# Entry of the two feed-forward blocks of a decoder trunk: order of the norm's sums, splits and deeper operands

## The chip, the cores and the metric

The kernel runs on one core of a Trainium2 chip. The metric is the device time of one execution in microseconds; a smaller number is better. The median of several runs is compared, and one further execution was profiled.

Names of engines: PE is the matrix engine (PEld its weight loads), DVE the vector engine, ACT the scalar engine, POOL GpSimd, SP the engine that issues most loads.

## The reference

Two layers on a residual stream x of 1024 tokens by 1024 features, all in float32. Layer 0 mixes tokens by a gated short convolution, layer 1 by attention with three dilated windows; each is followed by a SwiGLU feed-forward block with 2816 hidden features.

```python
h = rms_norm(x, mix_norm[i])
x = x + mixer(h, ...)                       # conv, then attention
h = rms_norm(x, ffn_norm[i])                # x * rsqrt(mean(x*x) + 1e-6) * gain
x = x + (silu(h @ w_gate) * (h @ w_up)) @ w_down
...
return rms_norm(x, final_norm)
```

## The kernel before

**Layout.** x is held transposed, as eight tiles X[0..7] of 128 features by 1024 tokens; a half is 512 tokens. Every float32 operand of a product is split into a high part (ACT copy, line 138) and a low part (DVE subtraction, line 139; lines 507 and 508 for the operands of the feed-forward block), and a product takes three matmuls per 128 by 128 block (hi·hi, hi·lo, lo·hi).

**Feed-forward block.** `Swiglu` multiplies the normed activations with the gate and up weights by Winograd's form of Strassen's method: seven products (u, m), m = 1..7, for each unit u of weight columns, over quarters of the activations (four feature tiles by one half of the tokens). Each product has 4 × 3 matmuls of 128 columns by 512 tokens (lines 515 to 517). The order is a written list, `unit_order` (line 252): for a feed-forward block it begins (0,1) (1,1) (0,2) (1,2) (2,1) (2,2) (3,1) (3,2) (0,6) (1,6) (0,7) (1,7) (0,4) (1,4) (0,5) (1,5) (0,3) (1,3) (2,6) ... with (3,4) as number 27. Below, "product n" is the n-th of that list. The operands of m = 1 and m = 2 need only the first half of the tokens (`first_half`, line 1061: `hcol`, line 1056, scales x by the gain and by 1/rms; then the split). Those of m = 3 to 7 need the second half too (`second_half`, line 1086, in six pieces): first the differences of scaled x tiles, times 1/rms, and so on. From unit 5 on, the products m = 2 and 4 are themselves cut by a second level of Winograd, on operands that `deepen` (line 619) prepares in some ten pieces out of the first level's (line 623 is its sums).

**What sets the order.** The program order of each engine's queue is the order in which Python emits the instructions; nothing is reordered. After product n `filled(n)` (line 766) calls `start(n)` (line 1141), then gives each of the running preparations (`deepen`) one step. Weight parts are `ops` in the order of use; `ensure(i)` (line 159) emits the loads and splits of all weights up to op i, `take` those of the product at hand and of one or two beyond.

**The entry.** The product ahead of a feed-forward block (`co`, the second half of the convolution's output projection, or `ao`, the last part of attention's) goes through `by_columns` (line 1170): first all eight output tiles for the first half of the tokens (j = 0; the first four, for `ao` five, with their products interleaved), then all eight for the second half (j = 1). After each tile: `add_to_x` (line 448) on DVE; `each`, that is `Norm.square` (line 397): ACT squares the half tile (line 408) and DVE adds the square of the tile before to `acc` (line 410); then `between` (line 1202), which saves X to DRAM, prepares weights and does these steps:

- j = 0: from tile 4 on, `ensure` of the first four weights of the feed-forward block; after tile 7 the last square is added, and DVE makes three weight sums (`combos`, line 186).
- j = 1, tile 0: `stats` part one: the column sums of `acc` on PE (line 427, eight one-column matmuls), square root on ACT (430), reciprocal and diagonal on DVE (431, 436). Tile 2: part two: spread over the partitions by PE (443) and ACT copy (444): 1/rms of the first half.
- j = 1, tiles 3 to 7: steps k = 0..7 of `first_half`, two at each of tiles 3 to 5, then one each. Each is followed by `gained(k)` (line 1073): ACT writes gain · x of the second half over the first half of X[k]; four differences of these (line 1084) are made on DVE.

In the feed-forward block `start` does the rest: product 0: end of `first_half`; 1: three sums and weights up to op (3,1); 2: `stats` part one for the second half; 3: part two and the first piece of `second_half`; 7, 8, 9, 11, 12: its other pieces. `deepen(2)` starts after product 12, `deepen(4)` after product 22 (lines 771, 773).

**End of attention.** `finish` (line 1473) divides the heads' outputs o by their sums z. For all pairs of heads but the last, z goes through DRAM, so that the reciprocal is of a 128 by 16 tile. For the last pair, DVE takes reciprocals of z in four pieces of 128 by 256 (line 1492), multiplies (1493), and splits each half of the tokens; this stands directly ahead of `ao`.

## Time and profile before

| | |
|---|---|
| median of 3 runs | 2200.58 us (2198.46 to 2203.82) |
| profiled execution | 2203.5 us, of which the profiled span is 2201.7 us |
| mean granted PE clock | 0.987 of full speed |
| feed-forward entry, layer 0 | about 305 to 420 us of the span |
| feed-forward entry, layer 1 | about 1485 to 1620 us |

A row of the timeline has the start, the duration, the engine, the line, the operation, output and inputs, and in brackets how long the engine had been idle before and what ended that. DVE instructions of one row overlap a little: 128 by 512 sums last 0.68 us and start every 0.60 us. A row of the windows view has for each stretch of the span the busy time of each engine with its count of instructions, the granted PE clock and the share and rate of the DMA engines.

### The profile page before, as it was taken

What the parts mean: (1) busy time and instruction counts of PE and PEld (TensorE: products, weight loads), DVE (VectorE), ACT (ScalarE), POOL (GpSimd) and SP (SyncE); (2) the same over time, 40 slices, a digit from 0 to 9 for tenths busy, and PEclk for the clock granted to TensorE, in tenths of its full rate; (3) what the DMA queues carried; (4) which work ended last, traced back from release to release, by engine and by line L of the source; (5) the groups of instructions that cost most, each with busy time, mean ns of one, the idle gap of its engine ahead of it and who ended that gap; (6) DMA issues with size and microseconds to landing.
All of it is one profiled execution on the core that took longest, in us unless ns stands there. A gap on an engine that the chain in (4) does not pass through costs nothing.

```text
span 2201.7 us, 30568 instructions
## 1 busy us (share of the span) xinstructions
PE 2143.2 (97%) x11158; PEld 1832.0 (83%) x11158; DVE 1762.2 (80%) x3242; ACT 997.6 (45%) x1800; POOL 153.2 (7%) x202
## 2 busy tenths in 40 slices
PE   9999999899999999999999999998899999999998
PEld 7788877688888878878999998887778888878887
DVE  7898759888888798865677777868988888889886
ACT  7433426444444444435455455534544444454435
POOL 1000000010101000010111111110010101000000
PEclk9999999999999999999999999999899999999999
DMA  7222631223333374323333333443123333265432
GB/s 222 82 91 68 224 121 39 91 96 106 110 97 119 123 280 147 113 67 130 91 91 92 94 98 89 153 148 132 53 79 105 104 105 112 96 233 198 158 91 77
DMA packets 132560, 260.03 MB, mean 118 GB/s; under 512 B 47530, under 2 KB 58810, under 8 KB 132410
## 3 DMA queue, kind: packets, MB, share of 16 engines
q1 hardware_dynamic: 76410, 186.38, 26.6%
q0 software_dynamic: 14832, 48.60, 6.4%
q10 hardware_dynamic: 41168, 23.10, 3.7%
q8 instruction: 88, 1.44, 0.3%
q14 instruction: 62, 0.51, 0.1%
HBM read 188.62 MB, written 66.26 MB: 116 GB/s over the span
## 4 chain that ended last, share of the span: by engine, by line
PE 80%; DVE 11%; ACT 4%; DMA 3%; issue 2%; ACTq 0%; SPq 0%; DVEq 0%
PE bank L517 16%; PE bank L515 16%; PE bank L516 16%; PE bank L356 5%; PE bank L358 5%; PE bank L357 5%; PE bank L1446 4%; PE bank L609 2%; PE bank L610 2%; PE bank L607 2%; DVE w L139 1%; DVE b L508 1%; PE bank L1374 1%; PE bank L1373 1%; DVE x L448 1%
## 5 line engine op out<-in xcount | busy, mean ns | idle before, releaser
L515 PE MATMUL bank<-b,w 128*128 128x512 f32 x1784 | 703.9, 395 | 14.3 <-ACT b L507 6.0
L517 PE MATMUL bank<-b,w 128*128 128x512 f32 x1784 | 702.1, 394 | 15.6 <-DVE w L139 15.6
L516 PE MATMUL bank<-b,w 128*128 128x512 f32 x1784 | 701.5, 393 | 2.6 <-DVE b L508 2.1
L517 PEld LDWEIGHTS bank<-b,w 128*128 128x128 f32 x1784 | 338.9, 190 | 91.0 <-DVE w L139 20.3
L515 PEld LDWEIGHTS bank<-b,w 128*128 128x128 f32 x1784 | 339.2, 190 | 88.5 <-ACT w L138 7.5
L516 PEld LDWEIGHTS bank<-b,w 128*128 128x128 f32 x1784 | 339.0, 190 | 73.8 <-DVE b L508 2.9
L138 ACT ACTIVATE w<-combo 128x512 fp32r<-128x512 f32 (+2 forms) x464 | 235.1, 535 | 289.2 <-DVE combo L186 280.2
L139 DVE TENSOR_TENSOR w<-combo,w 128x512 fp32r<-128x512 f32 (+2 forms) x464 | 261.3, 576 | 74.6 <-ACT w L138 71.9
L521 ACT ACTIVATE part<-bank 128x512 f32<-128x512 f32 x168 | 99.5, 595 | 271.9 <-PE bank L517 268.0
L139 DVE TENSOR_TENSOR w<-raw,w 128x512 fp32r<-128x512 f32 (+2 forms) x316 | 169.2, 561 | 21.1 <-ACT w L138 19.4
L525 DVE TENSOR_TENSOR part<-part,bank 128x256 f32<-128x256 f32 (+1 forms) x348 | 159.3, 488 | 28.9 <-PE bank L517 17.1
L138 ACT ACTIVATE w<-raw 128x512 fp32r<-128x512 f32 (+2 forms) x316 | 150.1, 520 | 45.5 <-PE bank L517 11.4
L736 DVE TENSOR_TENSOR x<-x,bank 128x512 f32<-128x512 f32 x168 | 114.6, 682 | 31.2 <-PE bank L517 31.2
L356 PE MATMUL bank<-w_hi,w 128*128 128x512 f32 (+1 forms) x320 | 121.5, 380 | 0.0
L358 PE MATMUL bank<-w_hi,w 128*128 128x512 f32 (+1 forms) x320 | 119.5, 373 | 0.7 <-DVE w L139 0.7
L357 PE MATMUL bank<-w_lo,w 128*128 128x512 f32 (+1 forms) x320 | 119.6, 374 | 0.0
L448 DVE TENSOR_TENSOR x<-x,bank 128x512 f32<-128x512 f32 (+1 forms) x104 | 66.0, 642 | 62.0 <-PE bank L358 53.0
L356 PE MATMUL bank<-h_hi,w_hi 128*128 128x512 f32 x256 | 104.6, 408 | 0.6 <-ACT w_hi L138 0.6
L186 DVE TENSOR_TENSOR combo<-raw 128x512 f32<-128x512 f32 (+1 forms) x160 | 103.2, 645 | 0.0
L358 PE MATMUL bank<-h_hi,w_lo 128*128 128x512 f32 x256 | 100.1, 391 | 0.8 <-DVE w_lo L139 0.8
L357 PE MATMUL bank<-h_lo,w_hi 128*128 128x512 f32 x256 | 99.9, 390 | 0.0
L1132 ACT ACTIVATE part<-part 128x512 f32<-128x512 f32 x66 | 39.7, 628 | 111.5 <-DVE part L525 111.5
(243 smaller groups left out, 3841.3 us busy)
## 6 DMA issues: line engine op xcount, KB each, us to landing
hin<-part SPq DMA_DIRECT2D x126, 256.0 KB
raw<-in_ffn_w_gate SPq DMA_DIRECT2D x44, 512.0 KB
raw<-in_ffn_w_up SPq DMA_DIRECT2D x44, 512.0 KB
part<-sum POOLq DMA_DIRECT2D x72, 256.0 KB, 3.0
raw<-in_ffn_w_down SPq DMA_DIRECT2D x48, 384.0 KB
raw<-in_conv_w_in SPq DMA_DIRECT2D x24, 512.0 KB
x<-spill SPq DMA_DIRECT2D x24, 512.0 KB
raw<-in_attn_w_qkv SPq DMA_DIRECT2D x24, 512.0 KB
```

Of the source, the lines that this page charges most:

```text
L138: nc.scalar.activation(hi, src, AF.Copy)
L139: eng.tensor_tensor(out=lo, in0=src, in1=hi, op=ALU.subtract)
L186: eng.tensor_tensor(out=c, in0=a, in1=b, op=op)
L356: nc.tensor.matmul(b, whi[:, a], ahi[:, s], start=first, stop=False)
L357: nc.tensor.matmul(b, whi[:, a], alo[:, s], start=False, stop=False)
L358: nc.tensor.matmul(b, wlo[:, a], ahi[:, s], start=False, stop=last)
L515: nc.tensor.matmul(b, hi[:, a], bhi, start=start and k == 0, stop=False, skip_group_check=True)
L516: nc.tensor.matmul(b, hi[:, a], blo, start=False, stop=False, skip_group_check=True)
L517: nc.tensor.matmul(b, lo[:, a], bhi, start=False, stop=k == n - 1, skip_group_check=True)
L521: nc.scalar.activation(t, b, AF.Copy)
L525: nc.vector.tensor_tensor(out=t, in0=t, in1=b, op=ALU.add)
L736: nc.vector.tensor_tensor(out=X[n][:, half(h)], in0=X[n][:, half(h)], in1=b, op=ALU.add)
```

## The change

It touches the entry of both feed-forward blocks and the end of attention.

1. `Norm.chained` takes the place of `Norm.square` there. Tile 0's square goes to `acc`, tile 1's to a second sum `odd`; those of tiles 2 and 3 are added to these two by accumulating DMAs on the POOL queue; those of tiles 4 to 7, and `odd`, by DVE: five DVE sums instead of seven in each half.
2. A new hook `added` runs between `add_to_x` and the square: the weights are split ahead of the square of the same tile, and two more (ops 4 and 5) are split in j = 1.
3. The three sums `combos` after j = 0 move behind part one of `stats`; part two moves from tile 2 to tile 1 of j = 1, and the steps of `first_half` become 0, 1, (2, 3), 4, 5, 6, 7 at tiles 1 to 7.
4. `gained` writes −gain · x for tiles 0 to 3 (the new constant `less`), and an accumulating DMA on the POOL queue adds tile k + 4 to tile k: the four DVE differences go.
5. `start`: each of the first steps moves ahead by one product, the pieces of `second_half` to products 2, 5, 7, 8, 9, 11. An activation on a scratch column asks for the Silu table after product 2; another for the Sqrt table at tile 4 of j = 0 (layer 1 only).
6. `deepen(2)` starts after product 17 (was 12), `deepen(4)` after 26 (was 22).
7. `finish`, last pair: the first half of the tokens as before; the second half's z goes to DRAM, comes back as 128 by 8, is inverted, goes to DRAM and is spread back, by five DMAs of the POOL queue; its multiplication and split (`last_part`) are emitted after tile 3 of `ao`, j = 0.

```diff
         def chained(self, k, c0, c1):
+            ...
+            if k == 1:
+                self.odd = half_page("acc2")
+            to = half_page("sq") if k > 1 else self.odd if k else acc
+            nc.scalar.activation(to, X[k][:, s], AF.Square)
+            add = lambda t: nc.vector.tensor_tensor(out=acc, in0=acc, in1=t, op=ALU.add)
+            if k in (2, 3):
+                nc.gpsimd.dma_start(out=(acc, self.odd)[k % 2], in_=to, accum_op=ALU.add)
+            if k == KT - 2:
+                self.flush()
+                add(self.odd)
+                self.odd = None
+            if k > 3:
+                self.flush()
+                self.put_off = lambda: add(to)
...
-                    if n == i - 15:
+                    if n == i - 10:
                         prep.append(self.deepen(2))
-                    if n == i - 5:
+                    if n == i - 1:
                         prep.append(self.deepen(4))
...
-            nc.scalar.activation(t, X[n][:, half(1)], AF.Identity, scale=self.norm.gain(n))
+            scale = (self.norm.gain(n), less[:, self.norm.g, n:n + 1])[n < 4]
+            nc.scalar.activation(t, X[n][:, half(1)], AF.Identity, scale=scale)
             self.xg[n] = t
-            if n > 4:
-                self.difference(n - 5)
+            if n > 3:
+                self.xd[n - 4] = self.xg[n - 4]
+                nc.gpsimd.dma_start(out=self.xd[n - 4], in_=t, accum_op=ALU.add)
...
                 if n == 0:
                     last_step()
-                elif n == 1:
                     for m in (6, 7):
                         combos[self.key, 1](m)
                     ensure(self.at(3, 1))
-                elif n == 2:
+                elif n == 1:
                     next(stats)
                     ensure(self.at(0, 6))
-                elif n == 3:
+                elif n == 2:
                     run(stats)
-                    ensure(self.at(1, 6))
                     prep.append(self.second_half())
                     next(prep[0])
-                elif n == 6:
+                    nc.scalar.activation(scratch, eps, AF.Silu)
+                    ensure(self.at(1, 6))
+                elif n == 4:
                     ensure(self.at(1, 7))
-                elif n in (7, 8, 9, 11, 12):
+                elif n in (5, 7, 8, 9, 11):
                     next(prep[0], None)
...
+            def added(j, n):
+
+                if j == 0 and n > 3:
+                    if n + 2 < KT:
+                        ensure(op_state[1] + 1)
+                    ensure(first_op + n - 4)
+                elif j and n < 2:
+                    ensure(first_op + n + 4)
...
                     if n == 3:
                         load_raw(raw_base[i] + 3)
-                    elif n > 3:
-                        ensure(first_op + n - 4)
-                    if n == KT - 1:
+                        if not i:
+                            nc.scalar.activation(less, gains, AF.Copy, scale=-1.0)
+                        if last_part:
+                            last_part.pop()()
+                    elif n == KT - 1:
                         norm.flush()
...
-                    for k in ((0, 1), (2, 3), (4, 5), (6,), (7,))[n - 3]:
+                    for k in ((0,), (1,), (2, 3), (4,), (5,), (6,), (7,))[n - 1]:
                         step(k)
...
+            nc.gpsimd.dma_start(wide(zd), z[0:65:64, HALF:])
+            zc = scope["pool"].tile([128, 8], F32, name="zl", tag="zl", bufs=1)
+            nc.gpsimd.dma_start(zc, thin(zd))
+            ...
+            for c in (0, 256):
+                nc.vector.reciprocal(z[:, c:c + 256], z[:, c:c + 256])
+                scaled(c, c + 256)
+                if c:
+                    parts(0)
                 yield
+            def rest():
+                scaled(HALF, S)
+                parts(1)
+            last_part.append(rest)
+            yield
+            nc.vector.reciprocal(zc, zc)
+            nc.gpsimd.dma_start(thin(rd), zc)
+            for a in range(2):
+                nc.gpsimd.dma_start(z[64 * a:64 * a + 64, HALF:],
+                                    bass.AP(rd.tensor, rd.offset + a * HALF, [[0, 64], [1, HALF]]))
+            yield
```

More of the change, by code (lines that the diff above doesn't have):

```diff
@@ L120, in trunk @@
     gains = consts.tile([128, 5, KT], F32)
+    less = consts.tile([128, 5, KT], F32)
     taps = consts.tile([128, KT, 3], F32)
@@ L418, in add, with chained @@
             self.square(k)
+        def chained(self, k, c0, c1):
+            s = slice(c0, c1)
+            if self.acc is None:
+                self.acc, self.rstd = page("acc"), page("rstd")
+            acc = self.acc[:, s]
+            if k == 1:
[12 more added lines that the diff above has]
+                self.put_off = lambda: add(to)
         def stats(self, c0, c1):
@@ L1168, in feed_forward, with by_columns @@
                 after(n)
-    def by_columns(key, ks, acts, pieces, each, between, wide=4, ahead=1):
+    def by_columns(key, ks, acts, pieces, each, between, wide=4, ahead=1, added=lambda i, n: None):
         w = {}
@@ L1185, in by_columns @@
                 add_to_x(n, banks[n])
+                added(i, n)
                 each(n, piece)
@@ L1206, in between @@
                         load_raw(raw_base[i] + 3)
-                    elif n > 3:
-                        ensure(first_op + n - 4)
-                    if n == KT - 1:
+                        if not i:
[3 more added lines that the diff above has]
+                    elif n == KT - 1:
                         norm.flush()
-                        for m in (6, 7):
-                            combos[i, 0](m)
-                    return
-                if n == 0:
+                    elif n == 4 and i:
+                        nc.scalar.activation(scratch, eps, AF.Sqrt)
+                elif n == 0:
                     pre.append(norm.stats(0, HALF))
                     next(pre[0])
-                if n == 2:
-                    run(pre.pop())
-                    pre.append(sw.first_half())
-                elif n > 2:
-                    for k in ((0, 1), (2, 3), (4, 5), (6,), (7,))[n - 3]:
+                    for m in (6, 7):
+                        combos[i, 0](m)
+                else:
+                    if n == 1:
+                        run(pre.pop())
+                        pre.append(sw.first_half())
+                    for k in ((0,), (1,), (2, 3), (4,), (5,), (6,), (7,))[n - 1]:
                         step(k)
-            by_columns((key, 1), ks, acts, HALVES,
-                       lambda n, c: norm.square(n, *c, eng=nc.vector), between,
-                       AO_WIDE if key == "ao" else 4)
+            by_columns((key, 1), ks, acts, HALVES, lambda n, c: norm.chained(n, *c), between,
+                       AO_WIDE if key == "ao" else 4, added=added)
         def last_step():
@@ L1230, in last_step @@
             norm.flush()
-            sw.difference(3)
         return sw, group1, norm.stats(HALF, S), last_step
@@ L1664, in trunk @@
         nc.tensor.matmul(warm[:, :128], ones, ones, start=True, stop=True)
+    last_part = []
     with tc.tile_pool(name="first", bufs=1) as scope["pool"]:
```

19 lines of the change are left out of this document (8 added, 11 removed).

## The prediction, written before the changed kernel was run

> **What bounds the kernel now.** I read the page first: its span, its table of engines and the shares of the chain that ended last.
>
> ```profile
> span 2201.7 us, 30568 instructions
> PE 2143.2 (97%) x11158; PEld 1832.0 (83%) x11158; DVE 1762.2 (80%) x3242; ACT 997.6 (45%) x1800; POOL 153.2 (7%) x202
> PE 80%; DVE 11%; ACT 4%; DMA 3%; issue 2%; ACTq 0%; SPq 0%; DVEq 0%
> ```
>
> PE bounds nearly everything: it idles 58.5 us in all. A change at two entries can win only what PE loses there, so the windows view over both comes second (busy time and count of PE, PEld, DVE, ACT, POOL, then the granted PE clock and DMA).
>
> ```profile
> 320.00:340.00 20.00, 18.67 (x77) 14.75 (x76) 12.94 (x21) 7.64 (x14) 0.00 (x0) 0.91 0.21 80
> 340.00:360.00 20.00, 18.76 (x85) 14.85 (x84) 18.77 (x33) 13.12 (x24) 0.00 (x0) 1.00 0.11 41
> 360.00:380.00 20.00, 20.00 (x90) 16.57 (x89) 19.84 (x33) 11.80 (x21) 0.00 (x0) 1.00 0.09 26
> 380.00:400.00 20.00, 14.35 (x55) 10.74 (x54) 18.92 (x35) 10.42 (x18) 1.62 (x3) 0.91 0.36 119
> 400.00:420.00 20.00, 16.42 (x64) 12.79 (x63) 18.12 (x31) 7.15 (x15) 2.69 (x5) 0.91 0.21 72
> 420.00:440.00 20.00, 20.00 (x89) 16.53 (x89) 15.77 (x29) 8.84 (x16) 0.96 (x2) 1.00 0.16 61
> 440.00:460.00 20.00, 20.00 (x89) 16.33 (x88) 17.33 (x33) 8.57 (x18) 2.27 (x5) 1.00 0.27 92
> ...
> 1500.00:1520.00 20.00, 15.58 (x63) 12.74 (x63) 14.90 (x25) 9.06 (x16) 0.00 (x0) 0.83 0.50 170
> 1520.00:1540.00 20.00, 19.08 (x83) 15.11 (x81) 17.32 (x28) 13.10 (x22) 0.00 (x0) 1.00 0.22 82
> 1540.00:1560.00 20.00, 18.83 (x70) 14.99 (x71) 17.15 (x30) 11.75 (x22) 0.00 (x0) 0.83 0.03 11
> 1560.00:1580.00 20.00, 18.46 (x82) 14.98 (x81) 19.07 (x32) 11.87 (x21) 0.00 (x0) 1.00 0.17 54
> 1580.00:1600.00 20.00, 15.95 (x57) 12.26 (x56) 19.14 (x36) 7.70 (x14) 2.17 (x4) 0.83 0.30 105
> 1600.00:1620.00 20.00, 17.53 (x71) 13.98 (x70) 15.80 (x29) 8.03 (x16) 2.16 (x4) 0.91 0.30 106
> ```
>
> Three readings. PE idles 1.33 + 1.24 + 5.65 + 3.58 = 11.8 us in entry 0 and 4.42 + 0.92 + 1.17 + 1.54 + 4.05 + 2.47 = 14.6 in entry 1. The clock is down by 3 × 0.09 × 20 = 5.4 us and (3 × 0.17 + 0.09) × 20 = 12.0. Together 43.8 us: the most there is to win. And DVE is at 18 to 20 of 20 just where PE idles, while at 420 to 460, at 15.8 and 17.3, PE has no gap. These are backlogs of DVE, each with an idle stretch of DVE ahead of it (12.9 at 320).
>
> The timeline gives the single gaps (in brackets):
>
> ```profile
> 321.75 1.05 PE L427 MATMUL bank<-ones,acc 128*128 128x1 f32 x8 [1.33 <-DVE acc L410]
> 392.30 0.50 PE L515 MATMUL bank<-b,w 128*128 128x512 f32 x1 [1.69 <-ACT w L138]
> 395.38 0.80 PE L517 MATMUL bank<-b,w 128*128 128x512 f32 x1 [2.35 <-DVE w L139]
> 395.98 0.63 PE L515 MATMUL bank<-b,w 128*128 128x512 f32 x1
> 396.41 0.63 PE L516 MATMUL bank<-b,w 128*128 128x512 f32 x1
> 414.67 0.50 PE L517 MATMUL bank<-b,w 128*128 128x512 f32 x1 [2.78 <-DVE w L139]
> ...
> 1513.46 1.87 PE L427 MATMUL bank<-ones,acc 128*128 128x1 f32 x8 [4.42 <-DVE acc L410]
> 1540.93 0.50 PE L516 MATMUL bank<-b,w 128*128 128x512 f32 x1 [1.85 <-DVE b L508]
> ```
>
> After the 2.35 gap matmuls start every 0.43 us; in the unbroken 20 us at 360 there are 90, one per 0.22 (0.227 from start to start in the timeline, used below). After the 1.69 gap they do not slow. So a gap somewhat above 2 us, or several close together, costs the clock too: this trace's rule, which I use for what stays.
>
> The Trainium skill, page "TensorE: Matmul & The Clock Gate", section "Part 1: The HAM clock gate", names about 3.4 us of idleness before the clock is halved. The trace disagrees: 2.35 us was enough. By the page only the 4.42 gap would take the clock with it (rival C).
>
> **The change part by part.** First the sums of j = 0:
>
> ```profile
> 313.30 0.68 DVE L448 TENSOR_TENSOR x<-x,bank 128x512 f32<-128x512 f32 x1
> 313.90 0.69 DVE L410 TENSOR_TENSOR acc<-acc,sq 128x512 f32<-128x512 f32 x1
> 315.26 0.69 DVE L139 TENSOR_TENSOR w<-raw,w 128x512 fp32r<-128x512 f32 x1 [0.68 <-ACT w L138]
> 315.87 0.68 DVE L448 TENSOR_TENSOR x<-x,bank 128x512 f32<-128x512 f32 x1
> ```
>
> A sum occupies DVE 0.60 us (313.30 to 313.90). A tile takes 2.57, of which 0.68 waits for ACT, whose split stands behind the square; PE makes a tile in 12 × 0.227 = 2.72, so DVE never catches up the 1.2 us it is behind. With the split ahead of the square the 0.68 goes: x, w, one sum is 1.8, with `odd` 2.4. PE was ready for L427 at 321.75 − 1.33 = 320.4, hence it had tile 7 at 317.7; tile 7's x, w and two sums end at 317.7 + 4 × 0.6 = 320.1. The 1.33 gap goes, with the slow clock behind it. ACT's queue now has the split ahead of the square, so late raw weights would hold the squares and the sums too; at 0.6 of each for ACT per 2.72 us there is room, and the raw tiles of these ops are loaded from tile 3 on as before. `less` is one ACT instruction in the same room.
>
> Entry 1 has the same chain, with 9 × 0.227 = 2.04 us per tile, and ahead of it the reciprocals:
>
> ```profile
> 1484.89 1.75 DVE L1492 RECIPROCAL z<-z 128x256 f32<-128x256 f32 x1
> 1486.74 0.42 DVE L1493 TENSOR_TENSOR o<-o,z 128x256 f32<-128x256 f32 x1
> 1516.61 1.28 ACT L430 ACT_TABLE_LOAD   x1
> ```
>
> Two reciprocals and multiplications (2 × 2.19) leave DVE before tile 0, but one multiplication and a split come back between tiles 3 and 4 (0.6, 0.6 waiting for ACT, 0.6), and the Sqrt table (1.28) now lies on ACT between tile 4's square and tile 5's split. PE was ready for L427 at 1513.46 − 4.42 = 1509.0; counting tiles back, it has tile 3 at 1500.2 (tiles 0 to 4 are interleaved, 0.68 apart). DVE: x3 to 1500.8, that detour to 1502.6, x4 and two splits to 1504.4, x5 to 1505.0. ACT, after x4 at 1503.2, has a square, the table, a root and a split, 0.6 + 1.3 + 0.3 + 0.6: 1506.0. Then DVE again: w, sum (1507.2), x, w, sum, odd (1509.6), x, w, two sums: 1512.0. The wait falls from 4.42 to 3.1 and keeps its slow clock (0.17 × 20): 3.1 + 3.4 = 6.5 us of loss stay here. From the chain of 1/rms itself the table load goes.
>
> The accumulating DMAs have no twin of their size. Bounds:
>
> ```profile
> acc<-sq POOLq DMA_DIRECT2D x6, 512.0 KB, 5.1
> part<-sum POOLq DMA_DIRECT2D x72, 256.0 KB, 3.0
> ```
>
> The first accumulates twice the bytes, the second copies the same; I take 5.1, the same operation. The POOL queue is empty in these windows (0.00), so nothing else is passed. Tile 2's square ends at about 307.5 and is needed at 314; in entry 1 at 1500.7 and 1506.6: both land in time, the second by 0.8. A late one would hold DVE at tile 5's sum, behind it x of tile 6, and with that a bank that PE needs. z's two trips are four hops in a row from 1484.9 on, when the first reciprocal has its z: at 3.0 each they end at 1496.9, at 5.1 at 1505.3; `rest` needs z at 1500.8. I take 3.0, since these hops copy and are smaller; at 5.1 DVE and all tiles behind it wait 4.5 us.
>
> Next the first half's norm and the first products. In entry 1 the column sums end at 1513.7 (1.7, as slow as in their row) and the diagonal at 1514.9. From there DVE has three weight sums, 7 x, 1 w, 8 hcol, 8 splits, 5 square sums: 24 × 0.60, and 8 a little dearer (gain and 1/rms in one, 0.66) = 19.7, so 1534.6, 1535.1 with what it waits for 1/rms. PE, from 1513.7: a slow tile, the spread, six tiles and two products = 3.3 + 0.9 + 12.2 + 5.4, so 1535.5. By 0.4 us neither L427 nor product 2 waits: the 1.85 at 1540.93 and the clock of its window go; in entry 0, with 2.72 a tile for PE, all the more, so the 1.24 idle at 340 to 360 goes too. At DVE a wait of L443's diagonal holds back only weight sums and x, which PE does not need at once.
>
> Last, the backlog in `second_half`, entry 0:
>
> ```profile
> 351.72 0.68 DVE L410 TENSOR_TENSOR acc<-acc,sq 128x512 f32<-128x512 f32 x1
> 360.54 2.49 DVE L1088 TENSOR_TENSOR x<-x,rstd 128x512 f32<-128x512 f32 x4
> 385.25 1.28 ACT L1132 ACT_TABLE_LOAD   x1 [1.43 <-issue]
> 392.70 1.42 DVE L623 TENSOR_TENSOR deep<-b 128x256 f32<-128x256 f32 x4
> 413.93 0.69 DVE L139 TENSOR_TENSOR w<-combo,w 128x512 fp32r<-128x512 f32 x1
> ```
>
> The last square sum, at 351.7, comes about 7 sooner: PE 3.1 (gap and clock), two sums 1.2, three differences 1.8, two early steps of `first_half` 1.9, less 1.0 waiting for PE. The weight splits of ops 4 and 5 fall into the 7 us that DVE idles at 320 to 340. Two splits and the fourth difference, 1.8, then make `second_half` start 8.8 sooner (360.54 to 351.7). `deepen(2)` is ten sums and splits of quarter width (0.34, by the row of four) and seven of full width: 7.6. Before, 5.7 of it preceded the split at 413.93, for product 20; now 1.3, so 4.4 move behind it. Silu's table load, which held up DVE behind ACT, comes right after 1/rms now and frees 0.6. In all 13.8: the split ends at 400.8. PE without gaps and slow clock is there at 414.67 − 11.8 − 3.6 = 399.3. So 1.5 of the 2.78 stays. `deepen(2)`'s other pieces now fall to products 18 to 24, where I leave as much again, and one slow window (1.8): 4.8 per entry, the same for entry 1. `deepen(4)` moves by four products, 11 us, into 440 to 460, where DVE had 2.7 of 20 us left: between 0 and its whole 7.6; I take 0, since its first user is product 37 and its last piece falls to product 33.
>
> Sum: 43.8 − 6.5 − 2 × 4.8 = 27.7. The profiled execution took 2203.5, so 2175.8; the median of the runs, 2200.6, is 2.9 below it, so **2173**.
>
> **The rivals.** B: DVE has no more room than the work taken from it. Four square sums and four differences per entry, 8 × 0.6 × 2 = 9.6, and 4.4 − 1.2 for the reciprocals: 12.8, so 2187.8. For it: 18 to 20 busy of 20 where PE idles. Against: DVE has 7 us idle at 320 to 340, and work moves there. A variant lets the late `deepen(4)` give back its 7.6 and a slow window of 1.8 per entry: 2173 + 19 = 2192.
>
> C: the clock does not come back with the short gaps. Then 26.4 − 3.1 − 4 × 1.5 = 17.3 of idleness is won alone: 2183.3. Against it: 360 to 380, no gap and clock 1.00.
>
> D, slower: the accumulates wait for DVE. The four differences enter the queue a tile of PE, 2.7 us, apart; the last, at about 344.4, beside the last square sum, is needed at 351.7. Its first user, product 8, comes 5 × 2.72 = 13.6 after 1/rms, and DVE needs 8.2 of these (4 scalings, 4 sums, 4 splits, 1.0 for ACT), so PE has 5.4 more. One behind another at T each they hurt by 4T − 3 × 2.7 − 7.3 − 5.4 = 4T − 20.8 per entry; with T = 12 that is 27, so 2173 + 54 = 2227. It eats the whole gain, 13.9 an entry, from T = 8.7 on. Against it: 3.0 and 5.1 were measured, the 3.0 in stretches where DVE had up to 19 of 20.
>
> The Trainium skill speaks for D: page "SBUF — State Buffer", section "A bandwidth-pool intuition that's wrong", has a POOL-issued DMA take 3100 ns instead of 620 while a DVE copy holds the shared port. No such stretch shows in the rows above.
>
> E: the change doesn't do what it says: every gap closed reappears at a later product: 2200.6.
>
> **How the numbers follow.** Forecast 0.62, B with its variant 0.24, C 0.03, E 0.05, D 0.06. A measurement tells 0.3% (6.6 us) from no change: faster 0.89, same 0.05, slower 0.06. The range runs from 2160, where the 16.1 us of loss that I leave shrink to 3, to B's 2192; it leaves out D, E and a little below: one in eight.
>
> **What would show it.** Right: no wait at L427 in entry 0 and 2 to 4 us in entry 1; none at L443; differences landing before L1088 starts; PE gaps of `w` at products 20 to 24 of at most 2 us; granted clock 1.00 from 1540 to 1580. Wrong: DVE waiting for a POOL-queue DMA (sums, differences or z), gaps at products 26 to 40, or PE idling as long as before with DVE at 19 of 20.

## The result, and the profile after

| | before | changed | |
|---|---|---|---|
| median (range), us | 2200.32 (2198.46 to 2203.82) | 2185.55 (2183.18 to 2186.07) | ratio 0.9929, 95% 0.9917 to 0.9942 |
| profiled execution's span, us | 2201.7 | 2184.3 | 17.4 less |

The kernel became 14.8 us faster; the forecast was 27.7 (2173). The lines of the page for the changed kernel that answer to those of before, the first with the span, then the engines, then the chain:

```profile
span 2184.3 us, 30619 instructions
PE 2134.3 (98%) x11158; PEld 1825.1 (84%) x11158; DVE 1750.1 (80%) x3224; ACT 999.7 (46%) x1804; POOL 169.8 (8%) x223
PE 78%; DVE 10%; ACT 4%; DMA 3%; issue 3%; ACTq 0%; SPq 0%; POOL 0%; DVEq 0%; POOLq 0%
```

PE still bounds it, and idles 50.0 us instead of 58.5. The windows of the changed kernel (busy time and count of PE, PEld, DVE, ACT, POOL, then PE's granted clock and DMA):

```profile
320.00:340.00 20.00, 20.00 (x88) 16.18 (x87) 17.34 (x28) 12.46 (x21) 3.38 (x4) 1.00 0.50 138
340.00:360.00 20.00, 20.00 (x91) 16.29 (x90) 18.10 (x32) 13.88 (x25) 1.69 (x2) 1.00 0.21 46
...
380.00:400.00 20.00, 18.09 (x79) 14.28 (x78) 19.07 (x34) 7.01 (x12) 4.40 (x8) 0.99 0.46 157
400.00:420.00 20.00, 20.00 (x84) 16.38 (x83) 15.44 (x28) 8.97 (x18) 0.45 (x1) 0.93 0.17 54
420.00:440.00 20.00, 19.06 (x84) 15.27 (x83) 18.35 (x34) 7.45 (x14) 2.80 (x6) 1.00 0.20 79
440.00:460.00 20.00, 17.74 (x104) 15.44 (x103) 16.81 (x40) 9.40 (x24) 0.54 (x1) 1.00 0.21 66
...
1480.00:1500.00 20.00, 17.63 (x78) 14.27 (x76) 11.33 (x20) 8.94 (x15) 4.02 (x6) 1.00 0.59 189
1500.00:1520.00 20.00, 16.75 (x65) 13.68 (x66) 16.99 (x28) 11.62 (x21) 1.68 (x2) 0.83 0.37 113
1520.00:1540.00 20.00, 18.85 (x86) 15.08 (x84) 18.67 (x32) 12.99 (x23) 3.36 (x4) 1.00 0.40 93
1540.00:1560.00 20.00, 19.44 (x85) 15.60 (x84) 20.00 (x34) 13.89 (x25) 0.00 (x0) 1.00 0.09 27
1560.00:1580.00 20.00, 20.00 (x88) 16.18 (x88) 19.00 (x31) 8.48 (x15) 3.60 (x7) 1.00 0.43 140
1580.00:1600.00 20.00, 18.09 (x73) 14.44 (x73) 15.85 (x31) 9.00 (x17) 0.80 (x2) 0.91 0.28 97
1600.00:1620.00 20.00, 19.06 (x84) 15.45 (x83) 19.33 (x35) 5.86 (x10) 3.25 (x6) 1.00 0.20 79
1620.00:1640.00 20.00, 17.74 (x98) 15.05 (x98) 16.02 (x37) 11.15 (x27) 0.54 (x1) 1.00 0.16 45
```

320 to 360, where PE idled and slowed before, is full at clock 1.00. New holes stand at 440 to 460 and 1620 to 1640, which were full. The timeline of the changed kernel names each gap (in brackets, with what ended it); lines moved by the change: L427 is L449, L443 is L465, L139 is L140, L515 to L517 are L537 to L539.

```profile
375.17 0.50 PE L539 MATMUL bank<-b,w 128*128 128x512 f32 x1 [0.55 <-DVE w L140]
399.40 0.75 PE L539 MATMUL bank<-b,w 128*128 128x512 f32 x1 [1.91 <-DVE w L140]
432.17 0.50 PE L539 MATMUL bank<-b,w 128*128 128x512 f32 x1 [0.94 <-DVE w L140]
448.01 0.50 PE L537 MATMUL bank<-b,w 128*128 128x512 f32 x1 [2.26 <-ACT part L543]
...
1503.25 1.01 PE L449 MATMUL bank<-ones,acc 128*128 128x1 f32 x4 [5.63 <-DVE acc L431]
1528.78 1.05 PE L449 MATMUL bank<-ones,acc 128*128 128x1 f32 x8 [1.15 <-DVE acc L431]
...
1583.47 0.50 PE L539 MATMUL bank<-b,w 128*128 128x512 f32 x1 [1.91 <-DVE w L140]
```

Counted in matmuls, the first four are products 12, 20, 31 and 36 (the expectations below call the third 34). Entry 1 repeats them (0.56, 1.91, 0.94, 2.26). With the clock's loss the entries now lose 5.66 + 1.6 (entry 0) and 12.44 + 5.2 (entry 1): 24.9 us, where the forecast left 16.1. Below, "first wait" and "second wait" are PE's waits for the column sums (L449) of the first and the second half of the tokens.

### The profile page after: what moved, and what is told of

Read it like the earlier page. It is cut to its first block, busy times and chain, and to the rows that moved or that the text cites. A ratio compares the mean times of both kernels' runs of the same rounds, so it can differ in the third digit from the quotient of the medians.

```text
span 2184.3 us, 30619 instructions
## 1 busy us (share of the span) xinstructions
PE 2134.3 (98%) x11158; PEld 1825.1 (84%) x11158; DVE 1750.1 (80%) x3224; ACT 999.7 (46%) x1804; POOL 169.8 (8%) x223
## 4 chain that ended last, share of the span: by engine, by line
PE 78%; DVE 10%; ACT 4%; DMA 3%; issue 3%; ACTq 0%; SPq 0%; POOL 0%; DVEq 0%; POOLq 0%
PE bank L537 15%; PE bank L539 15%; PE bank L538 15%; PE bank L359 5%; PE bank L357 5%; PE bank L358 5%; PE bank L1477 4%; PE bank L631 3%; PE bank L632 3%; PE bank L629 3%; DVE w L140 2%; PE bank L1405 1%; PE bank L1404 1%; DVE b L530 1%; DVE combo L187 1%
## 5 line engine op out<-in xcount | busy, mean ns | idle before, releaser
L537 PE MATMUL bank<-b,w 128*128 128x512 f32 x1784 | 702.9, 394 | 13.8 <-ACT part L543 6.6
L539 PE MATMUL bank<-b,w 128*128 128x512 f32 x1784 | 699.2, 392 | 9.3 <-DVE w L140 9.3
L537 PEld LDWEIGHTS bank<-b,w 128*128 128x128 f32 x1784 | 337.7, 189 | 88.3 <-ACT part L543 9.3
L539 PEld LDWEIGHTS bank<-b,w 128*128 128x128 f32 x1784 | 337.5, 189 | 84.7 <-DVE w L140 13.8
L139 ACT ACTIVATE w<-combo 128x512 fp32r<-128x512 f32 (+2 forms) x464 | 234.8, 535 | 291.8 <-DVE combo L187 282.8
L140 DVE TENSOR_TENSOR w<-combo,w 128x512 fp32r<-128x512 f32 (+2 forms) x464 | 261.0, 576 | 60.0 <-ACT w L139 57.6
L140 DVE TENSOR_TENSOR w<-raw,w 128x512 fp32r<-128x512 f32 (+2 forms) x316 | 169.4, 561 | 16.3 <-ACT w L139 14.8
L139 ACT ACTIVATE w<-raw 128x512 fp32r<-128x512 f32 (+2 forms) x316 | 150.7, 519 | 46.6 <-PE bank L539 13.6
```

The costliest lines, as they stand in the source:

```text
L139: nc.scalar.activation(hi, src, AF.Copy)
L140: eng.tensor_tensor(out=lo, in0=src, in1=hi, op=ALU.subtract)
L537: nc.tensor.matmul(b, hi[:, a], bhi, start=start and k == 0, stop=False, skip_group_check=True)
L539: nc.tensor.matmul(b, lo[:, a], bhi, start=False, stop=k == n - 1, skip_group_check=True)
```

## The experiments

Each edits the changed kernel alone and was timed in rounds beside the kernel before, whose median stayed between 2199.7 and 2201.4. One edited kernel's runs spread over 1.2 to 5.2 us, so I read nothing from under 2 us of difference to the changed kernel. That kernel was not timed again in these rounds: beside runs 5 to 8 the kernel before was 1.0 us slower than beside the changed kernel, so their last column may be 1 us too high.

| run | median (range), us | ratio to before (95%) | to the changed kernel |
|---|---|---|---|
| 1 deepen(4) back | 2179.96 (2179.57 to 2180.78) | 0.9909 (0.9895 to 0.9922) | -5.6 |
| 2 both deepens back | 2184.31 (2180.49 to 2185.17) | 0.9924 (0.9912 to 0.9936) | -1.2 |
| 3 z on DVE | 2184.54 (2183.84 to 2185.18) | 0.9930 (0.9916 to 0.9943) | -1.0 |
| 4 sums of tiles 2, 3 on DVE | 2187.16 (2183.15 to 2188.31) | 0.9937 (0.9924 to 0.9949) | +1.6 |
| 5 both 3 and 4 | 2183.19 (2181.56 to 2184.97) | 0.9918 (0.9905 to 0.9932) | -2.4 |
| 6 root's table earlier | 2185.37 (2183.45 to 2186.14) | 0.9926 (0.9914 to 0.9939) | -0.2 |
| 7 split behind the square | 2188.08 (2185.09 to 2188.61) | 0.9936 (0.9922 to 0.9949) | +2.5 |
| 8 differences on DVE | 2190.68 (2189.18 to 2190.93) | 0.9950 (0.9937 to 0.9962) | +5.1 |
| 9 first half's norm later | 2187.94 (2185.99 to 2189.75) | 0.9947 (0.9935 to 0.9960) | +2.4 |
| 10 high part a step ahead | 2182.31 (2180.73 to 2183.07) | 0.9921 (0.9907 to 0.9934) | -3.2 |
| 11 five edits together | 2176.63 (2174.60 to 2179.68) | 0.9893 (0.9878 to 0.9908) | -8.9 |
| 12 and two more | 2170.07 (2169.12 to 2171.73) | 0.9861 (0.9845 to 0.9878) | -15.5 |

**1 and 2: the deepen steps.** In `filled`:

```
-                    if n == i - 1:
+                    if n == i - 5:
                         prep.append(self.deepen(4))
```

> Edit: the changed kernel, with deepen(4) started at product 22 (index of the op less 5) again, as before the change; all else stays changed. Theory A (the 10 us that the forecast missed lie for the most part in deepen(4), moved by four products onto the early sums of unit 5): the waits of 0.94 and 2.26 us at products 34 to 36 of both entries go, at most 1.5 us per entry comes back at products 22 to 28, so 2 x 3.2 less 0 to 3: 3.4 to 6.4 us faster than the changed kernel, 2179 to 2182 us. Rival B (VectorE simply has no more room; the wait goes wherever deepen(4)'s 7.6 us are put): the same 3.2 per entry reappear as waits for w before product 30, time 2185 +- 2.

Run 2 also sets `i - 10` back to `i - 15` for `deepen(2)`.

> Edit: the changed kernel, with both deepen(2) (index less 15) and deepen(4) (index less 5) started where they were before the change. It prices the move of deepen(2) against the run with deepen(4) alone moved back. Theory A (the sooner sums and 1/rms gave VectorE 9 us ahead of product 12, so that deepen(2) would have had room in its old place for the most part): 4.4 us of its work return ahead of product 20's weights, the wait there grows from 1.9 us to 4 to 6 us with slow matmuls behind it, so 2 to 4 us per entry slower than with deepen(4) alone moved back: 2184 to 2190 us. Rival B (no room at all): all 4.4 us and a second slow window (1.8) per entry come back, about 12 us slower than that run: 2191 us or more.

The timeline of run 1, entry 0 from product 20 on, and the window that follows it:

```profile
399.33 0.50 PE L539 MATMUL bank<-b,w 128*128 128x512 f32 x1 [1.92 <-DVE w L140]
419.39 0.50 PE L539 MATMUL bank<-b,w 128*128 128x512 f32 x1 [0.71 <-DVE w L140]
424.05 0.50 PE L539 MATMUL bank<-b,w 128*128 128x512 f32 x1 [1.64 <-DVE w L140]
```

```profile
400.00:420.00 20.00, 19.29 (x86) 15.63 (x85) 17.61 (x35) 9.44 (x18) 0.00 (x0) 1.00 0.17 54
```

The 0.94 and 2.26 are gone, 0.71 and 1.64 stand in their place: theory A in the time, but 2.35 us per entry came back where it allowed 1.5. Of the 5.6 us by the medians, the two entries account for 3.5 in the profiles (1.9 idle time, 1.6 slow clock); the rest lies outside them, where the edit changes nothing (table below). `deepen(4)`'s move was a loss, then: 0.85 us of idleness an entry in these gaps, and the clock that goes with them. Run 2 is 4.4 slower than run 1, at A's end of the range: moving `deepen(2)` paid. Its product 20 waited 2.79 us, not the expected 4 to 6; products 15 to 17 waited 1.10, 1.20 and 0.86 ahead of it.

**3, 4, 5, 6: what holds entry 1's first column sums.** Run 3 puts `finish`'s old loop over four reciprocals back. Run 4:

```
             if k in (2, 3):
-                nc.gpsimd.dma_start(out=(acc, self.odd)[k % 2], in_=to, accum_op=ALU.add)
+                self.flush()
+                tgt = (acc, self.odd)[k % 2]
+                self.put_off = lambda: nc.vector.tensor_tensor(out=tgt, in0=tgt, in1=to, op=ALU.add)
```

> Edit: the changed kernel, with the last pair's z by four reciprocals of VectorE over 256 columns, as before the change; no DMAs of z, nothing left for between tiles 3 and 4. VectorE does two reciprocals more (1.75 each) before tile 0, and loses the waits for z's hops and the detour. Theory A (the hops came too late for the gain that they were to bring, and the detour between tiles 3 and 4 costs what the reciprocals cost): the first wait for the column sums in entry 1 is 5.6 +- 1.5 us, time 2185 +- 2. The forecast's own sum (hops in time, 4.4 less 1.2 us of VectorE saved): 3 us slower, 2188 to 2189. Rival (the late hops and the SWDGE traffic beside them are what holds the entry): the first wait falls below 4.4 us, 1.5 us or more faster.

> Edit: the changed kernel, with the sums of tiles 2 and 3 (squares) on VectorE instead of two accumulating DMAs, in both entries. It adds 2 x 0.60 us of VectorE per entry. Theory A (in entry 1 VectorE waited 0.77 and 0.59 us for these two DMAs, as much as the two sums take): entry 1's first wait 5.6 +- 0.7; entry 0's first wait comes back by at most 1.2; so 0 to 2 us slower than the changed kernel, 2185 to 2188. Rival D (the accumulating DMAs are what holds the entry): first wait of entry 1 below 4.5 us, 1 us or more faster.

Run 3's first wait is 6.26 us: taking the reciprocals off DVE was worth nothing measurable. Its timeline shows why, with the first of DVE's sums, that of tile 4's square, standing behind one DMA:

```profile
1495.51 0.69 DVE L431 TENSOR_TENSOR acc<-acc,sq 128x512 f32<-128x512 f32 x1 [3.56 <-DMA acc<-sq]
```

The changed kernel's DVE waits at both of these places too:

```profile
1496.82 0.69 DVE L431 TENSOR_TENSOR acc<-acc,sq 128x512 f32<-128x512 f32 x1 [0.77 <-DMA acc<-sq]
1499.91 0.69 DVE L431 TENSOR_TENSOR acc<-acc,acc 128x512 f32<-128x512 f32 x1 [0.59 <-DMA acc<-sq]
```

In that kernel the same transfers, in entry 0 (300 to 330; the third is the second half's) and in entry 1 (1475 to 1505), by its DMA issues (the last number is the median us to landing):

```profile
acc<-sq POOLq DMA_DIRECT2D x3, 256.0 KB, 3.2
```

```profile
acc<-sq POOLq DMA_DIRECT2D x2, 256.0 KB, 8.2
```

The second pair is late, and in run 3, without z's hops, took 8.0 as well: z's traffic is not what delays it. Run 4's first wait fell to 4.46, below what A allowed and just inside rival D's bound of 4.5, but the second rose from 1.15 to 2.35, and the time did not fall. Entry 0 shows no wait for these sums on DVE or PE in either kernel. So run 5 took both back:

> Edit: the changed kernel, with both the last pair's z (four reciprocals) and the sums of tiles 2 and 3 on VectorE; the deepen steps stay as changed. In the run with z alone on VectorE entry 1's first wait was 6.26 us, and VectorE waited 3.56 us for an accumulating DMA in it (the two took 8 us and more there). Theory A2 (in entry 1 the POOL-queue transfers, run beside the loads and spills, come later than the 3.0 to 5.1 us that the forecast took, and give back what they save VectorE): entry 1's first wait is 6.26 - 3.56 + 2 x 0.6 = 3.9 +- 0.6 us, the second 1.2 to 2.4; 1 to 3 us faster than the changed kernel (2185), 2182 to 2184. Rival B (VectorE's amount of work decides, and six operations come back to it): first wait 6 us or more, 2187 or more.

First wait 2.63 (A2: 3.3 to 4.5), second 2.77 (A2: 1.2 to 2.4): more was won at the first and more lost at the second than A2 said. The time is as A2 had it, though its 2.4 us hardly exceed the spread. What ended DVE's last wait there was the split behind the root's table load. Run 6 moved that load alone in the changed kernel:

```
             last_part.append(rest)
+            nc.scalar.activation(scratch, eps, AF.Sqrt)
             yield
```

> Edit: the changed kernel, with entry 1's early square root (the one that loads its table, 1.28 us on ScalarE) issued after the split of o's first half, where ScalarE idles 8 us, instead of behind tile 4's square. Theory A2 (that load held VectorE 1.07 us for a split, in the chain that ends at the first column sums): the first wait falls from 5.63 by 0.5 to 1.1 us, if the accumulating DMA, for which VectorE waited 0.77 right behind it, does not simply take its place; time 2184 to 2185. Rival (the DMA takes its place): first wait 5.3 or more, no change.

The DMA took its place: DVE waited 1.53 us for `acc<-sq` instead of 1.07 + 0.77, first wait 5.26, time unchanged. The rival (5.3 or more) held.

**7, 8, 9: parts that paid.** Run 7 swaps two calls in `by_columns`, so the next weights' split follows the square:

```
-                added(i, n)
                 each(n, piece)
+                added(i, n)
```

> Edit: the changed kernel, with the next weights' split issued behind the tile's square again instead of ahead of it. The forecast's own step (0.68 us of VectorE per tile waits for ScalarE when the split stands behind the square): from tile 4 on VectorE waits 0.68 per tile again; entry 0: a tile takes 2.5 (3.1 with the odd sum) against TensorE's 2.72, so the first wait comes back at 0.7 to 1.3 us; entry 1 (2.04 a tile): 4 x 0.68 less what lies in the waits for the accumulating DMAs (1.4), first wait 6.3 to 8.3 us. Time 2186 to 2189. Rival (the order is worth nothing, since the deferred sums fill that wait): no wait in entry 0, 5.6 in entry 1, 2185 +- 1.5.

Entry 0's first wait came back at 1.16 us, as the forecast's chain said; entry 1's stayed at 5.64 (expected 6.3 to 8.3): there DVE still waits 1.07 and 0.35 us for the DMAs, and for ACT twice (1.11 and 0.61) instead of at each of four tiles. Run 8 gives `gained` its old subtraction on DVE:

> Edit: the changed kernel, with the four differences of each entry on VectorE again (gains without the sign) instead of accumulating DMAs. It adds 4 x 0.60 us of VectorE per entry ahead of product 8. The forecast's step (they were 1.8 us, with the last one 2.4, of the backlog ahead of product 20): the wait at product 20 grows from 1.9 us by 1.8 to 2.4 us per entry, and product 13's from 0.55; 3 to 5 us slower than the changed kernel, 2188 to 2190. Rival D (the DMAs are what is late): no change or faster, 2185 or less.

The time nearly agrees (2190.7), the place does not:

```profile
344.03 1.05 PE L449 MATMUL bank<-ones,acc 128*128 128x1 f32 x8 [1.04 <-DVE acc L431]
...
400.31 0.50 PE L539 MATMUL bank<-b,w 128*128 128x512 f32 x1 [1.91 <-DVE w L140]
...
1531.01 1.87 PE L449 MATMUL bank<-ones,acc 128*128 128x1 f32 x8 [3.31 <-DVE acc L431]
```

Product 20 still waits 1.91. The 2.4 us of DVE work went to the second half's column sums (0 and 1.15 in the changed kernel). Run 9 moves the first half's 1/rms behind tile 2 and `first_half` to tile 3 on:

```
-                    if n == 1:
+                    if n == 2:
                         run(pre.pop())
                         pre.append(sw.first_half())
-                    for k in ((0,), (1,), (2, 3), (4,), (5,), (6,), (7,))[n - 1]:
-                        step(k)
+                    if n > 2:
+                        for k in ((0, 1), (2, 3), (4, 5), (6,), (7,))[n - 3]:
+                            step(k)
```

> Edit: the changed kernel, with the first half's 1/rms spread behind tile 2 of the second half (instead of tile 1) and first_half's eight steps from tile 3 on in their old groups (2, 2, 2, 1, 1). It moves about 1.9 us of VectorE's work per entry (the two early steps) behind the point where TensorE waits for the second half's column sums. Theory A2 (in entry 1 VectorE has no idle left between the two column sums; the run with the differences on VectorE shows what such work costs: +1.8 gave waits of 1.04 and 3.31 us there instead of 0 and 1.15): entry 0's second wait about 1, entry 1's 3.0 +- 0.5, product 20's unchanged at 1.9; 3 to 6 us slower than the changed kernel, 2188 to 2191. The forecast's own chain puts the 1.9 us into the backlog ahead of product 20: that wait 3.8 us instead of 1.9. Rival (VectorE's 2.7 us of idleness at 320 to 340 takes it): 2185 +- 1.5, nothing changes.

Second waits 0.55 and 3.14, product 20 at 1.95: A2's place again, and 2187.9, just under its range.

**10: is it the splits that make the later `deepen(4)` hurt?** Splits in `deepen` are cut: `parts` issues ACT's copies and returns DVE's subtractions, which run one step later:

```
-            d[6] = parts(t2, "half" if m == 2 else "page")
-            yield
-            d[7] = parts(t3, "page")
+            d[6], low = parts(t2, "half" if m == 2 else "page")
+            yield
+            low()
+            d[7], low = parts(t3, "page")
...
```

> Edit: the changed kernel, with the splits of the deepen pieces cut in two: ScalarE's high part is issued in one step, VectorE's low part one product later; the places of both deepens stay as changed. In the changed kernel VectorE waits 11.8 us in all for ScalarE in 12 such splits (none before the change, 5.5 with deepen(4) alone moved back): the high part stands on ScalarE behind an activation that itself waits for a sum of VectorE. Theory S (this wait, and not the 7.6 us of deepen(4)'s work, is what the later place costs, and what the forecast took as 0): VectorE's wait falls from 11.8 to below 3 us, the 2.26 us at product 36 falls below 1.3, 3 to 6 us faster than the changed kernel, 2179 to 2182. Rival W (the work itself collides with the eight early sums of unit 5): the waits at products 34 and 36 stay above 2.5 us together, 2184 to 2186.

The groups by line show DVE's part of these twelve splits (busy, mean ns | idle before them, and what ended it): before the change, in the changed kernel, in run 1 and in run 10.

```profile
L139 DVE TENSOR_TENSOR t<-deep,t 128x512 fp32r<-128x512 f32 x12 | 8.2, 684 | 0.0
```

```profile
L140 DVE TENSOR_TENSOR t<-deep,t 128x512 fp32r<-128x512 f32 x12 | 8.3, 691 | 11.8 <-ACT t L139 11.8
```

```profile
L140 DVE TENSOR_TENSOR t<-deep,t 128x512 fp32r<-128x512 f32 x12 | 8.2, 687 | 5.5 <-ACT t L139 5.5
```

```profile
L645 DVE TENSOR_TENSOR t<-deep,t 128x512 fp32r<-128x512 f32 x12 | 8.2, 685 | 0.0
```

In the changed kernel they cost DVE a microsecond each on average. Two rows of its timeline show one case: ACT itself has just waited for one of DVE's sums, and DVE then waits for the high part that ACT makes next:

```profile
445.20 0.63 ACT L1152 ACTIVATE part<-part 128x512 f32<-128x512 f32 x1 [4.72 <-DVE part L547]
446.38 0.69 DVE L140 TENSOR_TENSOR t<-deep,t 128x512 fp32r<-128x512 f32 x1 [1.22 <-ACT t L139]
```

Cutting the split takes all 11.8 us from these twelve splits, but not from DVE. The weights' splits of the same width, first in the changed kernel, then in run 10:

```profile
L140 DVE TENSOR_TENSOR w<-combo,w 128x512 fp32r<-128x512 f32 x224 | 153.7, 688 | 57.9 <-ACT w L139 57.6
L140 DVE TENSOR_TENSOR w<-raw,w 128x512 fp32r<-128x512 f32 x128 | 86.8, 686 | 14.8 <-ACT w L139 14.8
```

```profile
L140 DVE TENSOR_TENSOR w<-combo,w 128x512 fp32r<-128x512 f32 x224 | 153.8, 688 | 67.8 <-ACT w L139 67.5
L140 DVE TENSOR_TENSOR w<-raw,w 128x512 fp32r<-128x512 f32 x128 | 86.9, 686 | 17.1 <-ACT w L139 17.1
```

They wait 9.9 + 2.3 = 12.2 us more: the wait has moved to the next split. With both groups added, DVE waits for ACT for 90.8 us before the change, 84.2 in the changed kernel, 83.3 in run 1 and 84.6 in run 10. So run 10 does not show that this wait is what the later place costs. What it does change is the gaps: the 2.26 at product 36 goes, and product 31's 0.94 becomes 2.22. Together 3.20 an entry become 2.22, against 0.71 + 1.64 = 2.35 in run 1. The time, 2182.3, lies between S and W, and what separates it from run 1's is not in these gaps.

The gap at product 31 has a plainer origin. In the changed kernel its weights' split stands in DVE's queue directly behind two of `deepen(4)`'s sums, which run 1 has sooner:

```profile
430.10 1.41 DVE L645 TENSOR_TENSOR deep<-deep 128x512 f32<-128x512 f32 x2
431.43 0.69 DVE L140 TENSOR_TENSOR w<-combo,w 128x512 fp32r<-128x512 f32 x1
```

**11 and 12: together.** Run 11 joins 1, 3, 4, 10 and the table load (behind o's second split):

> Edit: the changed kernel with five edits together: deepen(4) at its old place, the splits of both deepens cut in two steps, z and the sums of tiles 2 and 3 on VectorE, and the early square root of entry 1 behind the second split of o. From the single runs: -5.6 (deepen(4)), -2 (z and sums: 2185.4 to 2183.2), up to -1.2 (VectorE's wait of 1.27 us for the table load, the next thing late once the accumulating DMAs are gone). Theory A2 (the effects lie at different places and add): 2175 to 2177; with theory S of the splits 2 to 4 us more, 2171 to 2175; entry 1's first wait 1 to 2 us, granted clock 1.00 there. Rival (what is won comes back at the second column sums or at products 20 to 26): 2179 or more.

2176.6, 8.9 us below the changed kernel: the single runs' effects add for the most part, and theory S's further 2 to 4 us do not come. Entry 1's first wait is 3.54, above the expected 1 to 2, with the clock at 0.90 and 0.93 instead of 1.00. The table load now holds the next split there: DVE waits 1.24 us for it, and then runs from 1483.26 to the column sums without one idle moment. Run 12 moves that load behind o's first split, and `deepen(2)` by one product:

```
-                    if n == i - 10:
+                    if n == i - 9:
...
-                    if h.start:
+                    if not h.start:
                         nc.scalar.activation(scratch, eps, AF.Sqrt)
```

> Edit: the kernel with the five edits together (2176.6), with two more at different places, which the trace keeps apart: deepen(2) one product later again (index less 9), and entry 1's early square root behind the first split of o, where ScalarE idles, instead of the second, where its table load held the next weights' split and with it VectorE for 1.24 us. The wait of 1.9 us at product 20 has stood in every run so far, whatever was done ahead of the second column sums. Theory P (it is set by what stands in VectorE's queue right ahead of that product's weights: four sums of a quarter, 2.5, then deepen(2)'s first piece, 1.35, then the weights' two sums and split): it falls by 1.35 to 0.6 us in both entries, with no slow matmuls behind it; the first wait of entry 1 falls from 3.5 to 2.3; time 2171 to 2174. Rival (a backlog of VectorE from second_half that the order of its last pieces doesn't change): the wait at product 20 falls, and the same 1.3 us return at products 21 to 24; time 2175 to 2177.

PE in run 12, entry 0 from product 20 on, and entry 1's first column sums (lines two further on, L541 for L539 and L451 for L449):

```profile
396.31 0.50 PE L541 MATMUL bank<-b,w 128*128 128x512 f32 x1 [0.59 <-DVE w L140]
419.22 0.50 PE L541 MATMUL bank<-b,w 128*128 128x512 f32 x1 [0.85 <-DVE w L140]
428.08 0.50 PE L541 MATMUL bank<-b,w 128*128 128x512 f32 x1 [0.41 <-DVE w L140]
...
1491.94 1.32 PE L451 MATMUL bank<-ones,acc 128*128 128x1 f32 x8 [1.99 <-DVE acc L431]
```

Product 20 falls from 1.92 to 0.59, as P says. Product 28 and 31 take back 0.95 of the 1.33 (0.85 + 0.41 against 0.31 in run 11), as its rival says, though at later products than the rival named. The time is P's, and lower: 2170.1, the fastest of all. No gap from product 12 on, at most 0.85 us, is followed by slow matmuls here. The table adds up from the windows PE's idle time and 20 us times what the clock lacks of 1.00, over both entries (300 to 460 and 1480 to 1660) and, both together, over the rest of the span, in us:

| | before | changed | run 1 | run 10 | run 11 | run 12 |
|---|---|---|---|---|---|---|
| entries: PE idle | 26.4 | 18.2 | 16.3 | 15.6 | 11.5 | 9.1 |
| entries: slow clock | 17.4 | 6.8 | 5.2 | 8.8 | 8.6 | 3.4 |
| rest: both | 44.6 | 43.6 | 39.1 | 40.7 | 42.5 | 39.6 |

The rest, which the edits hardly touch, differs by up to 4.5 us from the changed kernel's here (6.9 in run 8), mostly in slow clock: as much as most single edits are worth in time. So where an edit acts is read from the gaps, and its price in time is known only to a few microseconds. From run 11 to run 12, 2.4 us of the entries' gain are idle time and 5.2 clock. Of the clock, 1.8 belong to product 20 of entry 1; 3.4 belong to entry 1's column sums, where the first wait fell (3.54 to 1.99) and the second was alike (2.35 and 2.34). Run 11's profiled execution was also the slowest of its four (2179.7).

## Why the prediction was right in kind and half in size

Most of what it named in advance came: no wait at L449 in entry 0, none at L465, the differences landed ahead of `second_half`, the clock 1.00 from 1540 to 1580, PE's gaps at products 20 to 24 at most 1.91. But entry 1's first wait was 5.63 and not 2 to 4, and two of its three signs of being wrong came too: DVE waited for POOL-queue DMAs in entry 1, and gaps stood at products 31 and 36. Run 7 confirms the step on the split ahead of the square for entry 0. Rivals D and E fell: the differences by DMA are worth 4 to 5 us (run 8), not a loss, and no DVE wait for them shows.

The time, 2185.6, lies nearer to rival B's 2187.8 and rival C's 2183.3 than to the forecast; it is the width of the range that takes it in. What tells them apart is where the gain lies. C gives 17.3 us of idleness and no clock; the entries show 8.2 and 10.6. B pays only for work taken from DVE; but runs 7 and 9 change the order alone and bring waits back at entry 0's column sums (1.16 and 0.55 us), and run 5 gives DVE work back without a loss. That the total came out near theirs is chance.

Of the 8.8 us (24.9 - 16.1) that stay beyond the forecast, two terms of the sum hold all:

- "`deepen(4)` ... between 0 and its whole 7.6; I take 0": the mis-sized step. 0.94 + 2.26 = 3.2 us of idleness per entry, 6.4 in all, came with it, inside the bounds and a third of what the variant of rival B gave it (9.4 per entry). The reason given, that its user comes later, counted only its deadline and not what stands beside it in the queues. Run 1 shows that both gaps go with the later place, and also that the old place is not free: 2.35 per entry there. For product 31 the collision on DVE is seen (run 10's section); why product 36 waits 2.26 for ACT stays open.
- "The wait falls from 4.42 to 3.1 ... 6.5 us of loss stay here": it rose to 5.63 and kept its slow clock, 9.0 us. The step that failed is the accumulating DMA at 5.1 us; it took 8.2 there. DVE's waits for the two (0.77 + 0.59) and for z (0.36) are 1.7 of the 2.5 us beyond the forecast; the other 0.8 is not assigned. "Both land in time, the second by 0.8" was the thinnest margin of the sum. z's hops, at 5.0, 3.4, 1.7 and 2.8 us to landing, held DVE 0.36 us for the z that comes back, and 3.14 for the small one, which only ate into its wait for PE's first tiles (1.97 behind it). Run 5 shows the pair on DVE to be no worse. The table load named there held DVE 1.07 us, but run 6 shows that the DMA would have held it anyway.

The rest came to 9.5 us (0.55 + 1.91 + 1.6 in entry 0; 1.15 + 0.56 + 1.91 + 1.8 in entry 1) against 9.6, but not for the reason given, and the agreement is luck: the 1.15 at entry 1's second column sums, where the forecast had 0.4 us to spare, and the 0.55 at product 12 were not in it, while the second 1.5 per entry that it left for products 18 to 24 did not come. "In all 13.8: the split ends at 400.8" carried one backlog of DVE from the square sums to product 20. Runs 8 and 9 put DVE work into the stretch ahead of `second_half`, and product 20 waited 1.91 and 1.95 all the same. The changed kernel's DVE shows the break between the two:

```profile
350.16 2.50 DVE L1108 TENSOR_TENSOR x<-x,rstd 128x512 f32<-128x512 f32 x4 [1.58 <-ACT rstd L466]
```

DVE waits there for 1/rms, which comes by way of PE and ACT: a backlog ahead of it delays PE at the column sums and ends there. What product 20 waits for begins behind it, and run 12 shows that most of it, 1.33 of 1.92 us, is `deepen(2)`'s first piece standing ahead of that product's weights.

Not settled: why the two accumulating DMAs take 8 us in entry 1 and 3.2 in entry 0 (DMA's busy share is 0.59 against 0.42 there; no run changed the loads or spills beside them). The 18.8 us that idle time and clock of the entries give, with 1.0 of the rest, exceed the span's 17.4 by 2.4, which I did not trace.

## What to carry to other kernels

A piece of work moved later needs a look at what stands in the queues at its new place, not only at its deadline. A wait that goes from one group of instructions must be looked for in the next: run 10 took 11.8 us from one group of splits, and 12.2 came back at another. Where an engine waits for a result of the bounding engine, a backlog ahead of that point ends there; sum each side by itself. A transfer priced from rows of another stage wants a wide margin: 5.1 us was the row, 8.2 the fact, and 0.8 the margin. And when one edit is worth a few microseconds, compare the stretches that it does not touch, too: they differed by up to 6.9 us here.

## What the runs showed of the hardware

Whether a gap of 1 to 2.3 us slows TensorE's clock is not set by its length alone. At product 20 of entry 0, 1.91 us in the changed kernel was followed by eight slow matmuls (clock 0.93), 1.92 in run 1 by none (1.00). At product 36, 2.26 in the changed kernel was followed by none; run 4 (whose lines are two further on) has, after 2.25:

```profile
446.24 0.71 PE L539 MATMUL bank<-b,w 128*128 128x512 f32 x1 [2.25 <-ACT part L545]
446.75 0.63 PE L540 MATMUL bank<-b,w 128*128 128x512 f32 x1
447.18 0.63 PE L541 MATMUL bank<-b,w 128*128 128x512 f32 x1
...
449.74 0.42 PE L541 MATMUL bank<-b,w 128*128 128x512 f32 x1
```

Ahead of the column sums, whose eight one-column matmuls take 1.05 us, 1.04 us was followed by slow matmuls (run 8, entry 0, clock 0.91) and 1.15 by none (changed kernel, entry 1, 1.00). The slow stretch in run 4's lines lasts 3.5 us (446.24 to 449.74; 399.40 to 402.92 in the changed kernel) and costs half of that, the 1.8 of a window at 0.91. So the prediction's rule, "a gap somewhat above 2 us", falls. The Trainium skill, page "TensorE: Matmul & The Clock Gate", section "Part 1: The HAM clock gate", says that activity is judged over a free-running window of about 3.4 us, so that the same kernel can meet it at another phase. The stretch's length and the changing outcome agree with that; that about 3.4 us of idleness are needed does not, since 1.91 us were enough. Part of the differences between the kernels above is this draw. Run 2's five executions are of one kernel: the span was 2178.7 us at a mean granted clock of 0.994, 2180.3 at 0.993, and 2182.5 to 2183.4 at 0.992.
